# A decoder layer on one core: sixteen of the weight splits, and the gate factor of one branch, from VectorE to GpSimd

## The chip, the cores and the metric

The kernel runs on one core of a Trainium2 chip. The metric is the device time of one execution in microseconds (us). A core has TensorE (PE, matmuls, with its weight loads PEld), VectorE (DVE), ScalarE (ACT), GpSimd (POOL) and SyncE (SP, which here issues most DMA transfers). Each engine takes its instructions in the order in which they stand in its own queue and waits on semaphores for the others.

## The reference

One layer of a decoder trunk over 512 tokens of width 1024, all in float32:

```
h = rms_norm(x)
u = h @ w_in                     # 11512 columns: DSA, NSA, SSD inputs, three gates
y_a = dsa(u), y_b = nsa(u), y_c = ssd(u)     # three causal token mixers
mix = sig(g_a) * (y_a @ w_br_dsa) + sig(g_b) * (y_b @ w_br_nsa) + sig(g_c) * (y_c @ w_br_ssd)
x = x + mix @ w_out
x = x + square(relu(rms_norm(x) @ w_ff1)) @ w_ff2
```

DSA and NSA are attentions over selected keys (1024 wide each); SSD is a state-space mixer in four chunks of 128 tokens (2048 wide), and its output passes through an RMS norm with a gain of its own before the branch product.

## The kernel before

**Every product of matrices is three matmuls.** A float32 operand is split into a high half (rounded to the matmul's format, `F32R`) and a low half (the rest). `mm3` (L458 to L461) adds high x high, high x low and low x high in one PSUM bank. Activations are split once; weights are split as they stream in. The class `WS` holds the stream: a list of 190 and more weight pieces ("specs") in the order of use, each 128 x 1024 numbers at most. `load` fetches a piece into one of three raw buffers (`wraw`, issued on SP at L154); `split` makes the high half with a copy on ACT (L173) and the low half with a subtraction (L175), on DVE, except for the specs named in the set `LOWP`, whose low half POOL makes. The tiles `whi` and `wlo` have six buffers each, and splits run three specs ahead of use.

**The order of use.** Numbers of the specs: 0 to 67 are the projections of the mixers' inputs, 68 to 91 the 24 gate columns ("mg"), 92 to 99 the first branch (DSA output, a0), 100 to 107 and 108 to 115 the two halves of the third branch (SSD output, c0 and c1), then the second branch (NSA output, b0 and b1), `w_out` and the feed-forward weights.

**Two streams of work** are woven together: the mixers (DSA attention, then SSD, then NSA), whose matmuls are small and wait for softmaxes and exponentials, and the filler (projections, gates, branches), whose matmuls are 24 of 128x512 per output tile. The emission order is by a running balance of their costs; after that a scheduler with a model of each engine's times sets the order of instructions on every engine. So a change of engine for some instructions moves others too.

**SSD (about 400 to 570 us)** handles 16 units (group, chunk). For a unit POOL masks the decay exponents in a tile E (affine select, L1342), makes scaled inputs (xt L1347, xw L1350), adds (eab L1364), scales the state (hst L1373) and sums squares (yv, sq, L1390 and L1391). ACT takes exponentials of E (L1345), DVE multiplies E by a product that TensorE left in the single PSUM bank pv (L1352), and TensorE multiplies E with xt (L1312). After the NSA queries' norms POOL takes four powers (rs8, L1791). At the end four small matmuls (L1420) sum the squares, and the norm factors, one for each token, go through DRAM into the tile R (`rtok`), 128 x 512.

**The branches** (`branches`). For each of 8 output tiles m of a branch a gate tile (`gld`, 128 x 512, two buffers) is loaded by SP. It holds the hyperbolic tangent t; the sigmoid is (1 + t)/2, and the half is taken later. For the third branch the gate is first multiplied by the norm factor: `th = (th + 1) * R`, one instruction on DVE (L1564). TensorE makes the branch product p in a PSUM bank pj (two buffers), DVE takes `th * p` (L1589), and POOL adds this to the sum `mixf` (L1590), which frees the gate buffer. POOL also issues the loads of the queries for NSA (`qu <- q_d`, L1043, four buffers), each of which waits until TensorE has used the buffer's old contents.

Of the kernel before, what the change touches and what calls it, by code (L numbers as in the profile page):

```python
# [10 lines left out]
ALU = mybir.AluOpType  # L11
# [12 lines left out]
NS = 6  # L24
RAWB = 3
LEAD = 3
LOWP = {0} | set(range(8, 14)) | set(range(17, 24))
WE = 2
NH = 4
BH = 2  # L30
# [11 lines left out]
def build_kernel(ctx, tc, A, out):  # L42
    nc = tc.nc
    pe, act, dve, pool = nc.tensor, nc.scalar, nc.vector, nc.gpsimd
# [8 lines left out]
    def f(ap):  # L53
        return ap.bitcast(F32)
# [37 lines left out]
    def ps(tag, shape, dt=F32, bufs=2):  # L92
        if tag == XT[0]:
            XT[1] += 1
            if XT[1] % 3 == 0:
                tag = "pF"
        return psp.tile(shape, dt, tag=tag, name=tag, bufs=PSB[tag])
# [36 lines left out]
    class WS:  # L134
# [24 lines left out]
        def split(s):  # L159
# [14 lines left out]
            with tc.issue_after(H0[0][1]) if i == 1 else nullcontext():  # L174
                (pool if i in LOWP else dve).tensor_tensor(lo[:, :m], r[:, :m], f(hi[:, :m]), op=ALU.subtract)  # L175
            s.hl[i] = (hi[:, :m].rearrange("p (a b) -> p a b", b=w), lo[:, :m].rearrange("p (a b) -> p a b", b=w))
# [281 lines left out]
    def mm3(o, lh, ll, rh, rl, first, last):  # L458
        pe.matmul(o, lh, rh, start=first, stop=False)  # L459
        pe.matmul(o, lh, rl, start=False, stop=False)  # L460
        pe.matmul(o, ll, rh, start=False, stop=last)  # L461
# [39 lines left out]
    def proj_ch(i, rh, rl, p, first=True, last=True):  # L501
        wh, wl = ws.get(i)
        nk = ws.specs[i][1]
        for k in range(nk):
            mm3(p, wh[:, k, :], wl[:, k, :], rh(k), rl(k), first and k == 0, last and k == nk - 1)
            if k % 2 == 1:
                if k == nk - 1:
                    ws.free(i)
                yield 6 * 216
# [189 lines left out]
    def filler():  # L699
# [114 lines left out]
        while ya is None:  # L814
            yield None
            if "att2" in done:
                ya = first_ya()
        pclose("hT")
        yield from branches(ya)

    def load_y(yp, br, kk):
# [615 lines left out]
    def branches(ya):  # L1437
        bp = popen("br")
        mix = bp.tile([128, KT, S], F32, name="mixf")
        R = bp.tile([128, S], F32, name="rtok")  # L1440
# [9 lines left out]
        def load_g(n):  # L1450
            if n < len(seq) and n not in th_:
                br, m = seq[n]
                bi = "abc".index(br[0])
                c0, c1 = COLS.get(br, (0, S))
                if br[0] == "b":
                    gcnt[0] += 1
                g_ = R if br[0] == "b" and gcnt[0] % 3 == 0 else bp.tile([128, S], F32, name="gld", bufs=2)
                r0 = (bi * 8 + m) * 128
                if br in COLS:
                    g_ = g_.rearrange("p (a q) -> p a q", a=2)  # L1460
                    nc.sync.dma_start(g_, g_d[r0:r0 + 256, c0:c1].rearrange("(a p) q -> p a q", p=128))
                    th_[n], th_[n + 1] = g_[:, 0], g_[:, 1]
                else:
                    nc.sync.dma_start(g_, g_d[r0:r0 + 128])
                    th_[n] = g_

        def load(br, ks, pl):
            return [load_y(ypools[pl], br, kk) for kk in ks]
# [11 lines left out]
        for bi, br in enumerate(BR):  # L1480
# [54 lines left out]
            for m in range(8):  # L1535
                load_g(8 * bi + m)
                load_g(8 * bi + m + 1)
                if br in COLS and m % 2 == 0:
                    load_g(8 * bi + m + 2)
                    load_g(8 * bi + m + 4)  # L1540
                elif br == "b0":
                    load_g(8 * bi + m + 2)
                th = th_.pop(8 * bi + m)
                if br in ("a0", "c0", "c1") and m in (0, 6):
                    for m_ in (m, m + 1):
                        pp[m_] = ps("pj", [128, 512])
                    for half in range(2):
                        for m_ in (m, m + 1):
                            wi = P["br_" + br][m_]
                            wh, wl = ws.get(wi)  # L1550
                            for k in range(4 * half, 4 * half + 4):
                                mm3(pp[m_], wh[:, k, :], wl[:, k, :], yh[k], yl[k], k == 0, k == 7)
                            if half:
                                ws.free(wi)
                            yield 12 * 216
                        if m and not half:
                            nb_ = BR[bi + 1]
                            if nb_ == "c0":
                                while "yc" not in done:
                                    yield None  # L1560
                            if nb_ != "b0" or "nsa0" in done:
                                nxt = load(nb_, range(KS[nb_][0], KS[nb_][0] + 4), "A")
                if br[0] == "c":
                    dve.scalar_tensor_tensor(th, th, 1.0, R, op0=ALU.add, op1=ALU.mult)  # L1564
                if m in pp:
                    p = pp.pop(m)
                else:
                    p = ps("pj", [128, 512])
                    if br[0] == "b":
                        wi = P["br_b1" if br == "b2" else "br_" + br][m // 2]  # L1570
                        wh, wl = ws.get(wi)
                        ms = slice(128 * (m % 2), 128 * (m % 2) + 128)
                        for k in range(4):
                            mm3(p[:, :c1 - c0], wh[:, k, ms], wl[:, k, ms], yh[k][:, c0:c1], yl[k][:, c0:c1], k == 0, k == 3)
                            if k % 2:
                                if k == 3 and m % 2 and br != "b1":
                                    ws.free(wi)
                                yield 6 * (c1 - c0) / 2.37
                    else:
                        yield from proj_ch(P["br_" + br][m], lambda i: yh[i], lambda i: yl[i], p)  # L1580
                p = p[:, :c1 - c0]
                mx = mix[:, m, c0:c1]
                if br == "a0":
                    dve.scalar_tensor_tensor(mx, th, 1.0, p, op0=ALU.add, op1=ALU.mult)
                    continue
                if br[0] == "b":
                    dve.scalar_tensor_tensor(th, th, 1.0, p, op0=ALU.add, op1=ALU.mult)
                else:
                    dve.tensor_tensor(th, th, p, op=ALU.mult)  # L1589
                (dve if br in ("b1", "b2") else pool).tensor_tensor(mx, mx, th, op=ALU.add)  # L1590
                if br == "b2":
                    act.activation(mixh[:, m], mix[:, m], AF.Copy, scale=0.5)
                    dve.scalar_tensor_tensor(mixl[:, m], mix[:, m], 0.5, f(mixh[:, m]), op0=ALU.mult, op1=ALU.subtract)
# [264 lines left out]
```

## Time and profile before

| what | value |
|---|---|
| median of 3 runs | 1357.51 us (1356.02 to 1357.94) |
| the profiled execution | 1353.4 us |
| its span, first to last instruction | 1351.7 us |
| TensorE clock granted, mean | 0.995 |
| low halves on DVE, 128x1024 (raw piece from `wraw`) | 176, 223.6 us |
| low halves on POOL, 128x1024 | 9, 21.8 us |
| gate factors on DVE (L1564) | 16 |

The profile is of one execution. A row of an engine counts instructions that work on data; issuing a DMA, waiting and branching do not count as busy. A row names the line, the engine, the operation and `out<-in`. In a list of waits a row reads: the engine and tile that waited, the line, who released it, us in total, how many times, and the longest. A busy TensorE is not a TensorE at its peak, since the ends of matmuls are modelled. In a timeline, what stands in brackets is the engine's idle time ahead of the row and what ended it.

### The profile page before, as it was taken

To read this page: it belongs to the slowest core of one execution; us is meant where nothing else is said; L and a number is where in the kernel's file an instruction comes from. 1 tells how busy PE (TensorE), PEld (TensorE's weight loads), DVE (VectorE), ACT (ScalarE), POOL (GpSimd) and SP (SyncE) were. 2 spreads that over 40 slices of the span, in tenths; PEclk is the share of its full clock that TensorE was granted. 3 is DMA by queue.
4 is the path that set the end of the run, shared out by engine and by line. 5 is a ranking of instruction groups with operands and counts; after the bars stand their busy time and mean duration, and the time that the engine had idled before them with its cause. 6 is when DMAs were issued, how large, how long until landed. Compare 5 with 4: busy or idle time off the path is not lost.

```text
span 1351.7 us, 19620 instructions
## 1 busy us (share of the span) xinstructions
PE 1329.2 (98%) x6827; PEld 1111.0 (82%) x6827; DVE 994.2 (74%) x1971; ACT 728.3 (54%) x1395; POOL 272.0 (20%) x242
## 2 busy tenths in 40 slices
PE   9999999999999999999999999998999999999998
PEld 7788888888887777788888888887789888888887
DVE  6499986989977665467778889898655666767741
ACT  5455334677767775446665656556433443444420
POOL 2415111111006769500000112130000201102000
PEclk9999999999999999999999999999899999999999
DMA  6436665455559998663454545352427656746531
GB/s 199 120 88 170 189 179 137 123 159 144 146 149 347 304 295 289 193 187 102 118 164 119 167 136 145 117 168 94 156 66 188 132 160 132 179 114 127 150 125 47
DMA packets 251778, 213.74 MB, mean 158 GB/s; under 512 B 15882, under 2 KB 203166, under 8 KB 251679
## 3 DMA queue, kind: packets, MB, share of 16 engines
q1 hardware_dynamic: 235708, 188.88, 46.5%
q0 software_dynamic: 15232, 20.98, 8.2%
q10 hardware_dynamic: 738, 2.63, 0.5%
q8 instruction: 54, 0.88, 0.3%
q14 instruction: 46, 0.37, 0.1%
HBM read 171.75 MB, written 40.70 MB: 157 GB/s over the span
## 4 chain that ended last, share of the span: by engine, by line
PE 86%; DVE 4%; POOL 3%; ACT 2%; DMA 2%; issue 2%; SPq 0%; DVEq 0%; ACTq 0%; POOLq 0%
PE pj L459 20%; PE pj L460 20%; PE pj L461 20%; PE sc L461 3%; PE sc L459 3%; PE sc L460 3%; PE pT L984 3%; PE pv L997 2%; PE pv L996 2%; PE sc L925 2%; PE sc L924 2%; PE sc L1312 1%; POOL rs L1791 1%; DVE wlo L175 1%; PE pF L984 1%
## 5 line engine op out<-in xcount | busy, mean ns | idle before, releaser
L173 ACT ACTIVATE whi<-wraw 128x1024 fp32r<-128x1024 f32 (+2 forms) x190 | 198.3, 1046 | 238.0 <-PE pj L460 121.4
L175 DVE TENSOR_TENSOR wlo<-wraw,whi 128x1024 fp32r<-128x1024 f32 (+1 forms) x176 | 223.6, 1272 | 104.2 <-ACT whi L173 101.2
L459 PE MATMUL pj<-hTh,whi 128*128 128x512 f32 x512 | 203.5, 397 | 2.0 <-DVE cacc L853 2.0
L460 PE MATMUL pj<-hTl,whi 128*128 128x512 f32 x512 | 202.4, 395 | 0.0
L461 PE MATMUL pj<-hTh,wlo 128*128 128x512 f32 x512 | 202.2, 395 | 0.0
L933 ACT ACTIVATE p<-p,nb,rs 128x256 f32<-128x256 f32 (+3 forms) x160 | 107.8, 677 | 45.9 <-DVE nb L931 45.7
L459 PEld LDWEIGHTS pj<-hTh,whi 128*128 128x128 f32 x512 | 96.3, 188 | 20.9 <-ACT eab L1341 2.2
L460 PEld LDWEIGHTS pj<-hTl,whi 128*128 128x128 f32 x512 | 96.4, 188 | 19.2 <-issue 1.0
L461 PEld LDWEIGHTS pj<-hTh,wlo 128*128 128x128 f32 x512 | 96.3, 188 | 19.0 <-issue 0.2
L460 PE MATMUL pj<-yl,whi 128*128 128x512 f32 (+1 forms) x288 | 107.9, 375 | 0.0
L459 PE MATMUL pj<-yh,whi 128*128 128x512 f32 (+1 forms) x288 | 107.1, 376 | 0.8 <-ACT yh L1477 0.4
L461 PE MATMUL pj<-yh,wlo 128*128 128x512 f32 (+1 forms) x288 | 106.8, 372 | 0.0
L460 PE MATMUL pj<-h2l,whi 128*128 128x512 f32 (+1 forms) x256 | 96.4, 377 | 0.0
L461 PE MATMUL pj<-h2h,wlo 128*128 128x512 f32 (+1 forms) x256 | 96.3, 376 | 0.0
L459 PE MATMUL pj<-h2h,whi 128*128 128x512 f32 (+1 forms) x256 | 96.2, 377 | 0.0
L459 PE MATMUL pj<-whi,hTh 128*128 128x512 f32 (+2 forms) x208 | 80.0, 385 | 3.2 <-DVE v_s L561 2.2
L460 PE MATMUL pj<-wlo,hTh 128*128 128x512 f32 (+2 forms) x208 | 80.4, 387 | 0.0
L461 PE MATMUL pj<-whi,hTl 128*128 128x512 f32 (+2 forms) x208 | 79.8, 384 | 0.0
L988 ACT ACTIVATE pth<-pT 128x512 fp32r<-128x512 f32 x95 | 54.7, 592 | 43.5 <-PE pT L984 42.7
L1043 POOL DMA_DIRECT2D qu<-q_d x32 | 23.5, 736 | 264.4 <-PE sc L925 186.5
L989 DVE TENSOR_TENSOR ptl<-pT,pth 128x512 fp32r<-128x512 f32 x95 | 63.7, 679 | 4.4 <-ACT pth L988 4.3
L459 PE MATMUL sc<-whi,fh 128*128 128x512 f32 x168 | 65.4, 389 | 0.0
(410 smaller groups left out, 3155.7 us busy)
## 6 DMA issues: line engine op xcount, KB each, us to landing
wraw<-in_w_in_dram SPq DMA_DIRECT2D x84, 512.0 KB, 4.2
wraw<-in_w_ff_dram SPq DMA_DIRECT2D x58, 512.0 KB, 4.1
qd<-in_w_ff_dram POOLq DMA_DIRECT2D x18, 512.0 KB, 5.9
gld<-g_d SPq DMA_DIRECT2D x35, 256.0 KB, 2.7
q_d<-qev SPq DMA_DIRECT2D x64, 128.0 KB, 3.6
qu<-q_d POOLq DMA_DIRECT2D x32, 256.0 KB, 4.8
E<-ac_d SPq DMA_DIRECT2D x16, 512.0 KB, 6.1
xz<-xzt_d SPq DMA_DIRECT2D x16, 512.0 KB, 4.4
```

The lines of the kernel that those rows point to most:

```text
L173: act.activation(hi[:, :m], r[:, :m], AF.Copy)
L175: (pool if i in LOWP else dve).tensor_tensor(lo[:, :m], r[:, :m], f(hi[:, :m]), op=ALU.subtract)
L459: pe.matmul(o, lh, rh, start=first, stop=False)
L460: pe.matmul(o, lh, rl, start=False, stop=False)
L461: pe.matmul(o, ll, rh, start=False, stop=last)
L924: pe.matmul(s_[:, h % w, :n], u.q[h], kh[:, :n], start=True, stop=False)
L925: pe.matmul(s_[:, h % w, :n], u.q[h], kl[:, :n], start=False, stop=True)
L933: act.activation(u.p[h][:, :n], u.p[h][:, :n], AF.Exp, bias=u.nb[:, h:h + 1], scale=rs8[:, u.b, u.h0 + h:u.h0 + h + 1], accum_out=u.sm[:, ...
L984: pe.transpose(pt[:, h], u.p[h][:, kb * 128:kb * 128 + 128], ident)
L988: act.activation(ph, ptf, AF.Copy)
L989: dve.tensor_tensor(pl, ptf, f(ph), op=ALU.subtract)
L996: pe.matmul(o, vk, ph0, start=st, stop=False)
```

## The change

```diff
-LOWP = {0} | set(range(8, 14)) | set(range(17, 24))
+LOWP = {0} | set(range(8, 14)) | set(range(17, 24)) | set(range(70, 116, 3))
...
                 if br[0] == "c":
-                    dve.scalar_tensor_tensor(th, th, 1.0, R, op0=ALU.add, op1=ALU.mult)
+                    pool.tensor_tensor(th, th, R, op=ALU.mult)
+                    pool.tensor_tensor(th, th, R, op=ALU.add)
```

First, the low half of specs 70, 73, ... 115, sixteen in all, is made by POOL and not by DVE: 8 of the gate columns, 2 of the first branch and 6 of the third. Second, the third branch's gate times norm factor is made on POOL, by two instructions, `th * R` and then `+ R`, for each of its 16 tiles. Lines behind L1564 have numbers one higher in the new file. The instructions before and after each are the same, but the scheduler gives all engines another order from about 500 us on.

POOL in the second half of SSD, before; E_5160 is the decay tile of one unit, xt_5256 belongs to the unit before, rs8 are the four powers:

```order
L1390 TENSOR_TENSOR yv_5151<-yv_5151 128x256
L1364 TENSOR_TENSOR eab_5113<-eab_5113,xz_5051 128x512
L1391 TENSOR_TENSOR sq0_4087<-sq0_4087,yv_5151 128x256
L1347 TENSOR_TENSOR xt_5256<-xs_5162,sv_dth_1818 128x512
L1373 TENSOR_TENSOR hst_5135<-hst_5135,sv_dec_1821 128x512
L1350 TENSOR_TENSOR xw_5320<-xs_5236,sv_dw_1820 128x512
L1364 TENSOR_TENSOR eab_5168<-eab_5168,xz_5109 128x512
L1342 AFFINE_SELECT E_5160<-E_5160 128x1024
L1791 TENSOR_TENSOR rs8_316<-ssn_317,mhalf_164 128x16 x4
```

The same place after the change, from the add eab_5113 on:

```order
L1364 TENSOR_TENSOR eab_5113<-eab_5113,xz_5051 128x512
L175 TENSOR_TENSOR wlo_6038<-wraw_5816,whi_6037 128x1024
L1347 TENSOR_TENSOR xt_5256<-xs_5162,sv_dth_1818 128x512
L1792 TENSOR_TENSOR rs8_316<-ssn_317,mhalf_164 128x16 x4
L1390 TENSOR_TENSOR yv_5151<-yv_5151 128x256
L1373 TENSOR_TENSOR hst_5135<-hst_5135,sv_dec_1821 128x512
L1364 TENSOR_TENSOR eab_5168<-eab_5168,xz_5109 128x512
L1350 TENSOR_TENSOR xw_5320<-xs_5236,sv_dw_1820 128x512
L1347 TENSOR_TENSOR xt_5318<-xs_5236,sv_dth_1818 128x512
L1391 TENSOR_TENSOR sq0_4087<-sq0_4087,yv_5151 128x256
L175 TENSOR_TENSOR wlo_6244<-wraw_6041,whi_6243 128x1024
L1342 AFFINE_SELECT E_5160<-E_5160 128x1024
```

The powers moved from behind the select of E_5160 to ahead of it, xt_5318 too, and two splits came in ahead of it (a third, wlo_5813, stands five rows above those shown).

POOL in the third branch, before; the numbers of `gld` tell the gate tiles apart, `qu` are query loads:

```order
L1043 DMA qu_8127<-q_d3_2_71 128x2x256
L1043 DMA qu_8129<-q_d3_2_71 128x2x256
L1590 TENSOR_TENSOR mixf_7585<-mixf_7585,gld_8224 128x512
L1590 TENSOR_TENSOR mixf_7585<-mixf_7585,gld_8248 128x512
L1590 TENSOR_TENSOR mixf_7585<-mixf_7585,gld_8393 128x512
L1590 TENSOR_TENSOR mixf_7585<-mixf_7585,gld_8398 128x512
L1590 TENSOR_TENSOR mixf_7585<-mixf_7585,gld_8465 128x512
L1043 DMA qu_8933<-q_d3_1_70 128x2x256
```

And after, from the second add of a gate's norm factor on:

```order
L1565 TENSOR_TENSOR gld_8248<-gld_8248,rtok_7586 128x512
L175 TENSOR_TENSOR wlo_8548<-wraw_8296,whi_8547 128x1024
L1591 TENSOR_TENSOR mixf_7585<-mixf_7585,gld_8224 128x512
L1591 TENSOR_TENSOR mixf_7585<-mixf_7585,gld_8248 128x512
L1564 TENSOR_TENSOR gld_8394<-gld_8394,rtok_7586 128x512
L1564 TENSOR_TENSOR gld_8400<-gld_8400,rtok_7586 128x512
L1043 DMA qu_8129<-q_d3_2_71 128x2x256
L1565 TENSOR_TENSOR gld_8394<-gld_8394,rtok_7586 128x512
L1565 TENSOR_TENSOR gld_8400<-gld_8400,rtok_7586 128x512
L1591 TENSOR_TENSOR mixf_7585<-mixf_7585,gld_8394 128x512
```

A query load that stood ahead of all adds of the branch now stands between the multiplies and the adds of two gate tiles, and splits stand among them.

## The prediction

> **What bounds the kernel now.** I read the page first, then the busy time by stage, then what TensorE waits for in each stage, then the chain of waits around the places that the change touches. The page:
>
> ```profile
> span 1351.7 us, 19620 instructions
> PE 1329.2 (98%) x6827; PEld 1111.0 (82%) x6827; DVE 994.2 (74%) x1971; ACT 728.3 (54%) x1395; POOL 272.0 (20%) x242
> ```
>
> TensorE is busy for all but 22.5 us, so the whole kernel is a queue of matmuls, and a gain can come only from those gaps. I cut the span where the work changes: 490 to 570 us is the end of the SSD mixer, 570 to 690 gate projections beside NSA attention, 690 to 850 the first and third branch beside NSA, 850 to 970 the second branch and the end of NSA. Columns: us, PE, PEld, DVE, ACT and POOL busy with counts, clock, DMA.
>
> ```profile
> 490.00:570.00 80.00, 78.05 (x435) 62.21 (x436) 47.81 (x57) 47.68 (x99) 62.34 (x48) 1.00 0.80 257
> 570.00:690.00 120.00, 120.00 (x609) 100.55 (x609) 84.29 (x235) 70.97 (x152) 5.79 (x8) 1.00 0.48 140
> 690.00:850.00 160.00, 159.94 (x823) 135.24 (x821) 138.01 (x324) 98.17 (x196) 20.82 (x17) 1.00 0.50 143
> 850.00:970.00 120.00, 111.64 (x638) 96.76 (x637) 103.87 (x278) 71.42 (x165) 19.61 (x15) 0.96 0.40 122
> ```
>
> From 570 to 850 us, where 12 of the 16 moved splits and nearly all the moved gate factors lie, TensorE idles for 0.06 us, although VectorE is 86% busy (138.01 of 160) in the second half. Freeing VectorE there cannot shorten anything directly. The gaps lie before and after, and the waits of TensorE name them, first 490 to 570 us, then 850 to 970 us (us in total, times, longest).
>
> ```profile
> PE pv L1312 <- DVE E L1352: 0.7, 1, 0.7
> PE pF L619 <- DVE qev L623: 0.6, 1, 0.6
> PE sc L1312 <- DVE eab L1363: 0.4, 1, 0.4
> ```
>
> ```profile
> PE pv L996 <- ACT pth L988: 2.1, 1, 2.1
> PE pv L1152 <- DVE yr L1007: 2.0, 1, 2.0
> ...
> PE pv L1152 <- DVE yt L1014: 0.7, 1, 0.7
> ...
> ```
>
> So 1.7 us are open in the SSD stage and 4.8 us in these three rows of the tail. One sign that VectorE is near to mattering in between: the chain of waits passes through its queue from about 797 us and gives TensorE a start at 820.77 with nothing to spare.
>
> ```profile
> 818.32 0.84 DVE wlo L175
> 819.44 0.67 DVE gld L1564
> 820.11 0.61 DVE gld L1589
> 820.77 0.50 PE pj L459
> ```
>
> **The change part by part.** What one of each costs, first the low halves (ns least/median/largest on DVE; on POOL busy us and mean ns), then the gate factor on DVE, and the nearest POOL row to its replacement, an add of two 128x512 fp32 tiles in SBUF.
>
> ```profile
> L175 DVE TENSOR_TENSOR wlo<-wraw,whi x176: 1097/1220/3486, 11.0 to 1324.7; 128x1024 fp32r<-128x1024 f32 x173, 128x912 fp32r<-128x912 f32 x3
> L175 POOL TENSOR_TENSOR wlo<-wraw,whi 128x1024 fp32r<-128x1024 f32 x9 | 21.8, 2437 | 37.2 <-ACT whi L173 36.7 <-POOL wlo L175 0.6
> L1564 DVE SCALAR_TENSOR_TENSOR gld<-gld,rtok x16: 670/678/694, 755.7 to 872.6; 128x512 f32<-128x512 f32 x16
> L1590 POOL TENSOR_TENSOR mixf<-mixf,gld x22: 1281/1295/2276, 765.6 to 920.0; 128x512 f32<-128x512 f32 x22
> ```
>
> Sixteen splits leave DVE: 16 x 1.22 = 19.5 us; on POOL they are 16 x 2.44 = 39.0 us. Sixteen factors leave DVE: 16 x 0.68 = 10.8 us; on POOL each is a multiply and an add, 16 x 2 x 1.295 = 41.4 us. DVE loses 30.3 us, POOL gains 80.4 us. None of it is on TensorE's path as long as TensorE's waits stay as they are, so the sum is made of what happens to those waits, stage by stage.
>
> SSD stage (490 to 570 us). Five splits (specs 70, 73, 76, 79, 82) come onto POOL here, 5 x 2.44 = 12.2 us into 17.7 us of idle time (80 less 62.34). The order puts three of them, the four powers and one more multiply (xt) ahead of the select that makes E_5160. The rows that time this today, POOL, DVE and PE:
>
> ```profile
> 512.87 1.54 POOL L1342 TENSOR_SCALAR_AFFINE_SELECT E<-E 128x1024 f32<-128x1024 f32 x1
> 514.39 12.51 POOL L1791 TENSOR_TENSOR rs<-ssn,mhalf 128x16 f32<-128x16 f32 x4
> 528.24 1.04 POOL L1347 TENSOR_TENSOR xt<-xs,sv_dth 128x512 f32<-128x512 f32 x1
> ```
>
> ```profile
> 517.79 1.21 DVE L1352 TENSOR_TENSOR E<-E,pv 128x1024 f32<-128x1024 f32 x1
> ```
>
> ```profile
> 519.81 0.38 PE L1312 MATMUL pv<-bcx 128*128 128x128 f32 x2
> 526.70 1.09 PE L1312 MATMUL sc<-E,xt 128*64 128x128 f32 x16 [0.41 <-DVE eab L1363]
> ```
>
> ```profile
> 1150.00:1200.00 50.00, 50.00 (x222) 41.45 (x221) 36.01 (x40) 22.23 (x25) 4.91 (x4) 1.00 0.61 148
> ```
>
> Today the select starts at 512.87, its product with the decay (read from the one pv bank) ends at 519.0, and TensorE's next matmul into that bank stands at 519.81: 0.8 us to spare. After the change the select is behind 12.5 (powers) + 1.0 (xt) + 3 x 2.44 (splits) = 20.8 us more: near 533.7, and its product ends 6.1 us on, at 539.8. TensorE gets there later too: counted from the last row that both orders share, 130 projection matmuls stand ahead of that pv matmul where 50 stood, 80 x 0.225 us (50 us over 222) = 18.0 us, so at 537.8. That is a wait of 2.0 us in place of 0.8 us to spare, less what POOL's gaps take in (17.7 us are idle in the stage). Bounds: -1.7 us if all three waits of the stage go, +7.6 us if the three splits are also stretched as the worst add was (2276 over 1295 ns in the row above, 3 x 2.44 x 0.76 = 5.6 us). I take +1.0 us, between the 2.0 and the 0.7 of today's wait of the same kind (pv behind the product), to which it is nearest.
>
> Middle (570 to 850 us). The weights: a POOL split ends about 1.2 us later than a DVE split, and so frees its raw buffer later; three splits of lead, each 24 matmuls of 0.225 us (5.4 us), cover that, and on SP the load of the next raw tile and what is queued behind it (gate loads, stores of attention output) move by the same 1.2 us under the same cover. The gates: one gate buffer's round is load, factor, product, add, and the load is the page's row:
>
> ```profile
> gld<-g_d SPq DMA_DIRECT2D x35, 256.0 KB, 2.7
> ```
>
> Before 2.7 + 0.68 + 0.68 + 1.3 = 5.4 us, now 2.7 + 2.6 + 0.68 + 1.3 = 7.3 us, for two buffers 3.6 us per output tile against 5.4 us of matmuls per tile: hidden. What can bring it out is POOL's order. POOL also issues the query loads, and one of those (qu_8129) now stands between the multiplies and the adds of two gates. It waits for TensorE to free a query buffer, and such waits are long (570 to 850 us):
>
> ```profile
> POOL qu L1043 <- PE sc L925: 128.8, 6, 28.6
> ```
>
> Today nothing urgent is queued behind them. Now a late query load holds the add, the add holds the product on DVE (L1590 of the new file waits for POOL), and behind that product stand NSA's maxima and exponent biases. Against that, DVE gets slack. How much of it stays is told by how the two engines run side by side, DVE then POOL:
>
> ```profile
> 765.71 4.62 DVE L175 TENSOR_TENSOR wlo<-wraw,whi 128x1024 fp32r<-128x1024 f32 x2
> ```
>
> ```profile
> 765.57 2.53 POOL L1590 TENSOR_TENSOR mixf<-mixf,gld 128x512 f32<-128x512 f32 x2
> ```
>
> Two splits that cost 2.44 us alone took 4.62 us beside two POOL adds of 2.53 us: DVE lost 2.2 us, nearly all of POOL's time. DVE's instructions of this kind, two inputs in SBUF, from 570 to 850 us:
>
> ```profile
> L175 DVE TENSOR_TENSOR wlo<-wraw,whi 128x1024 fp32r<-128x1024 f32 x35 | 44.8, 1283 | 11.3 <-ACT whi L173 10.9 <-DMA g_d<-gth 0.3
> L829 DVE SCALAR_TENSOR_TENSOR yl<-yl,gcol,yh 128x512 fp32r<-128x512 f32 x16 | 12.3, 783 | 1.6 <-ACT yh L828 1.6
> ```
>
> With 11 splits left on POOL here (11 x 1.28 = 14.1 us off the first row) these two rows are 43.0 us of 280, 15%. POOL's new 41.4 + 11 x 2.44 = 68 us then block DVE for about 0.15 x 68 = 10 us, out of 14.1 + 10.8 = 24.9 us won: some 40% is handed back. [...] The page "Perfetto Trace Analysis" of the Trainium skill, section "Optimizing Scalar/DVE Operations", warns that for this reason moving work between the two might not help; by that rule the sum of this stage would be nil or a loss. By the rows it is nil too, since nobody waits for DVE here: bounds 0 and the loss under the rivals; I take +0.
>
> Tail (850 to 970 us). No split or factor of this stage moves, but the order on TensorE does. Now 29 branch matmuls of 128x256 stand in TensorE's order between the last score matmuls (L946) and the pv matmuls that wait (L1152); after the change 48, the same matmuls otherwise. Their pace (24 rows, first and last), the last scores and the waits:
>
> ```profile
> 929.38 0.28 PE L459 MATMUL pj<-yh,whi 128*128 128x256 f32 x1
> 932.12 0.28 PE L461 MATMUL pj<-yh,wlo 128*128 128x256 f32 x1
> 935.99 0.28 PE L946 MATMUL sc<-kl_j,qu 128*128 128x256 f32 x1
> 942.89 0.72 PE L984 MATMUL pF<-ident,p 128*128 128x128 f32 x3 [1.37 <-DVE p L970]
> 944.33 0.50 PE L1152 MATMUL pv<-cph,vz 128*128 128x256 f32 x2 [0.72 <-DVE yt L1014]
> 948.45 0.48 PE L1152 MATMUL pv<-cph,vz 128*128 128x256 f32 x2 [1.99 <-DVE yr L1007]
> ```
>
> 19 x 2.74/23 = 2.3 us more cover for waits of 1.37 + 0.72 + 1.99 = 4.1 us that follow from those scores through softmax, transposes and yr. Bounds 0 (what limits them is queued elsewhere) and -2.3 us; I take half, -1.1 us.
>
> Sum: +1.0 + 0 - 1.1 = -0.1. The profiled execution took 1353.4 us, 1.7 us beyond its span; by the sum it would take 1353.3. The runs shown have a median of 1357.51, 4.1 us above it, and I set the change against that: 1357.4 us.
>
> **The rivals.** (1) Faster: the 1.7 us of SSD waits go, because two of the three are waits for DVE's queue, which loses splits there, and the tail gets its full 2.3 us: -4.0 us, 1353.5. For it speaks that each wait named is on DVE; against it, the powers and splits now ahead of the select.
> (2) Slower, in the middle: POOL becomes late. The place is the product L1590 of the new file, 16 times, with NSA's chain behind it and TensorE without slack as at 820.77. If each costs TensorE 0.5 us, +8 us, 1365.5. It decides from the point where DVE's loss eats its gain: blocking above 24.9/68 = 37% of POOL's new time (15% by the rows above), or query loads that hold an add longer than the 5.4 us of one tile. For it: 138.01 of 160 us busy on DVE, and the queue order. Against it: POOL would still be only near 80 of 160 us busy.
> (3) Slower, in the SSD stage: the splits on POOL are stretched by DVE beside them, and TensorE waits 2.0 us and half of the 5.6 us for the pv bank, nothing coming back before the next stage: with the tail at -1.1, +3.7 us, 1361.2. For it: POOL is 78% busy there (62.34 of 80) before 12.2 us are added. Against it: the order has already moved 80 matmuls in front.
>
> **How the numbers follow.** A change of under 0.2% (2.7 us) is about what a measurement of this kernel can tell from none. My forecast, within that, 0.40; rival 1 0.30; rival 2 0.15; rival 3 0.15. So faster 0.30, same 0.40, slower 0.30. The forecast's own range is 1354.8 to 1360. The range for 8 in 10 reaches to both near rivals, 2 us past rival 1 for a tail whose first wait (2.1 us) goes too, and into the lower half of rival 2: 1351.5 to 1363.5.
>
> **What would show it right or wrong.** Right: TensorE idle again near 22 us, nil between 570 and 850; POOL busy near 350 us; DVE busy down by 15 to 25 us and not by 30, with L175 on DVE beside POOL stretched; a wait of pv or sc L1312 near 535 us of at most 2 us; the waits before L1152 shorter. Wrong: TensorE waits with a DVE product or POOL gld as releaser between 690 and 850 us (rival 2), one wait of 4 us or more near 535 us (rival 3), or a tail without its two or three waits (rival 1).

## The result, and the profile after

| | median, us | runs |
|---|---|---|
| before | 1356.76 (1353.84 to 1357.94) | 4 |
| after | 1371.70 (1368.88 to 1377.24) | 4 |
| ratio | 1.0118, 95% interval 1.0079 to 1.0158 | |

The change makes the kernel slower by 1.2%, some 15 us, where the forecast was no change and the range ended at 1363.5 us. A second series of the same kernel gave 1.0123 (1.0107 to 1.0139). The profiled execution took 1373.88 us, so the two profiles lie somewhat farther apart (20.5 us) than the medians (14.9 us). Its page:

```profile
span 1372.2 us, 19644 instructions
PE 1336.8 (97%) x6827; PEld 1110.6 (81%) x6827; DVE 997.0 (73%) x1939; ACT 729.5 (53%) x1395; POOL 351.4 (26%) x290
```

POOL is where the prediction put it (351.4 us, forecast near 350). DVE is not: 30 us of work left it and its busy time rose from 994.2 to 997.0 us. TensorE idles 1372.2 - 1336.8 = 35.4 us where it idled 22.5, so 12.9 of the 20.5 us by which the span grew are open gaps. The other 7.6 us count as busy, for the same 6827 matmuls at a mean clock of 0.996 (0.995 before). Added up, the durations of these matmuls are 2469.0 us before and 2469.6 us after, so the matmuls are not longer: they overlap less. A matmul that is listed at 0.39 us follows the one before it after 0.225 us (50 us over 222 matmuls), so a wait of under some 0.17 us opens no gap. That the 7.6 us are such short waits is a guess that no run here tests.

The same stretches as before (us, then PE, PEld, DVE, ACT and POOL busy):

```profile
490.00:570.00 80.00, 75.80 (x436) 60.51 (x433) 43.93 (x48) 47.28 (x98) 63.97 (x49) 1.00 0.83 258
570.00:690.00 120.00, 119.25 (x603) 99.64 (x602) 81.32 (x213) 67.98 (x143) 23.24 (x18) 1.00 0.48 139
690.00:850.00 160.00, 150.26 (x749) 124.46 (x748) 129.43 (x294) 91.93 (x189) 59.23 (x41) 0.99 0.46 132
850.00:970.00 120.00, 111.69 (x612) 93.02 (x610) 107.78 (x276) 72.16 (x171) 41.42 (x30) 0.99 0.41 123
```

Idle time grew by 2.25 us in the SSD stage (from 1.95 to 4.20), by 0.75 from 570 to 690, by 9.7 in the middle (from 0.06 to 9.74), and not at all in the tail (8.31 against 8.36). The stage in which I had costed everything at nothing made most of the new idle time. Who ended TensorE's longest waits from 690 to 990 us (total, times, longest):

```profile
PE sc L924 <- DVE mx L926: 4.2, 5, 1.9
PE pj L459 <- DVE gld L1590: 3.0, 1, 3.0
PE pv L1152 <- DVE yr L1007: 2.8, 1, 2.8
PE pv L997 <- DVE ptl L989: 2.0, 4, 1.4
PE pj L460 <- DVE yl L829: 1.7, 2, 1.0
```

In these five rows every releaser is DVE; the next one is a wait of 1.5 us for ACT (pth, 2.1 us before). Three of the five are new, the tail's wait for yr was there with 2.0 us, and that for ptl with 0.6:

```profile
PE pv L997 <- DVE ptl L989: 0.6, 1, 0.6
```

DVE in turn waits for POOL's gate in only one place from 690 to 870 us:

```profile
DVE gld L1590 <- POOL gld L1565: 1.4, 1, 1.4
```

That wait ended at 784.40 us, and TensorE has no idle time between 771 and 804 us. So a late POOL queue is not what TensorE waits for. What slows DVE is seen in the durations of instructions that nobody moved. First before, then after, 690 to 990 us, by shape (busy us, mean ns):

```profile
L175 DVE TENSOR_TENSOR wlo<-wraw,whi 128x1024 fp32r<-128x1024 f32 x35 | 47.3, 1354 | 2.6 <-ACT whi L173 2.5
L829 DVE SCALAR_TENSOR_TENSOR yl<-yl,gcol,yh 128x512 fp32r<-128x512 f32 x16 | 12.3, 783 | 1.6 <-ACT yh L828 1.6
L931 DVE SCALAR_TENSOR_TENSOR nb<-mx,rs 128x4 f32<-128x4 f32 x19 | 3.4, 179 | 0.2
```

```profile
L175 DVE TENSOR_TENSOR wlo<-wraw,whi 128x1024 fp32r<-128x1024 f32 x26 | 42.1, 1617 | 0.0
L829 DVE SCALAR_TENSOR_TENSOR yl<-yl,gcol,yh 128x512 fp32r<-128x512 f32 x16 | 16.8, 1068 | 5.0 <-ACT yh L828 5.0
L931 DVE SCALAR_TENSOR_TENSOR nb<-mx,rs 128x4 f32<-128x4 f32 x19 | 9.2, 483 | 0.3
```

Nine splits left DVE here (35 to 26), and only 5.2 us went with them (47.3 to 42.1). The third row is the one to look at. `nb` is the exponent's bias of an NSA unit, 128x4 numbers, a link of the chain scores, maximum (L926), bias (L931), exponential on ACT (L933). It took 0.18 us on average and takes 0.48. One of them, DVE and then POOL:

```profile
791.08 2.14 DVE L931 SCALAR_TENSOR_TENSOR nb<-mx,rs 128x4 f32<-128x4 f32 x1
```

```profile
790.82 2.37 POOL L175 TENSOR_TENSOR wlo<-wraw,whi 128x1024 fp32r<-128x1024 f32 x1
```

POOL's split began 0.26 us earlier and ended at 793.19; the little instruction ended at 793.22. It did 0.15 us of work (its median before is 150 ns) and stood for the rest of POOL's instruction, and the exponentials stood behind it. Six of the 19 took over 0.25 us after the change (one before), and each of the six began while POOL was inside a split, a multiply of a gate or an add to `mixf`.

This one held up no matmul: TensorE isn't idle near 793 us. The longest wait of the middle, 3.0 us, has the same picture in front of it. TensorE, then DVE, then POOL:

```profile
770.86 0.50 PE L459 MATMUL pj<-yh,whi 128*128 128x512 f32 x1 [3.00 <-DVE gld L1590]
```

```profile
767.38 2.10 DVE L1127 TENSOR_SCALAR ib<-ib 128x8 f32<-128x8 f32 x1
769.52 0.69 DVE L1130 TENSOR_TENSOR smask<-ib,caus 128x512 f32<-128x512 f32 x1
770.12 0.68 DVE L1590 TENSOR_TENSOR gld<-gld,pj 128x512 f32<-128x512 f32 x1
```

```profile
767.10 2.35 POOL L175 TENSOR_TENSOR wlo<-wraw,whi 128x1024 fp32r<-128x1024 f32 x1 [1.65 <-ACT whi L173]
```

An instruction on 128x8 numbers, 0.17 us before the change, stood until POOL's split ended, and the product that TensorE's matmul waits for stood behind it. It has one tensor input, so not only instructions with two are held up. Of TensorE's seven waits of more than 0.1 us between 690 and 850 us (9.7 us together) five, with 6.9 us, have such a held-up DVE instruction at most two rows ahead of the releaser or as the releaser itself (L1127, L175 and three of yl L829). Ahead of the other two, 1.9 and 0.8 us, DVE had itself been idle for 1.6 and 2.4 us, waiting for ACT's yh.

### The profile page after: what moved, and what is told of

Read it like the earlier page. It is cut to its first block, busy times and chain, and to the rows that moved or that the text cites. A ratio compares the mean times of both kernels' runs of the same rounds, so it can differ in the third digit from the quotient of the medians.

```text
span 1372.2 us, 19644 instructions
## 1 busy us (share of the span) xinstructions
PE 1336.8 (97%) x6827; PEld 1110.6 (81%) x6827; DVE 997.0 (73%) x1939; ACT 729.5 (53%) x1395; POOL 351.4 (26%) x290
## 4 chain that ended last, share of the span: by engine, by line
PE 85%; DVE 7%; DMA 3%; ACT 2%; issue 2%; POOL 0%; SPq 0%; DVEq 0%; ACTq 0%; POOLq 0%
PE pj L459 20%; PE pj L460 20%; PE pj L461 20%; PE sc L459 3%; PE sc L461 3%; PE sc L460 3%; PE pT L984 2%; PE sc L924 2%; PE sc L925 2%; PE pv L996 2%; PE pv L997 2%; PE sc L1312 1%; DVE wlo L175 1%; ACT p L933 1%; DMA yl<-yc_d 1%
## 5 line engine op out<-in xcount | busy, mean ns | idle before, releaser
L175 DVE TENSOR_TENSOR wlo<-wraw,whi 128x1024 fp32r<-128x1024 f32 (+1 forms) x160 | 208.0, 1301 | 93.4 <-ACT whi L173 91.2
L933 ACT ACTIVATE p<-p,nb,rs 128x256 f32<-128x256 f32 (+3 forms) x160 | 108.3, 680 | 72.5 <-DVE nb L931 72.4
L175 POOL TENSOR_TENSOR wlo<-wraw,whi 128x1024 fp32r<-128x1024 f32 (+2 forms) x30 | 68.6, 2292 | 125.5 <-ACT whi L173 125.0
L459 PEld LDWEIGHTS pj<-yh,whi 128*128 128x128 f32 x288 | 55.1, 192 | 14.3 <-DVE gld L1590 3.1
```

The lines of the kernel that those rows point to most:

```text
L933: act.activation(u.p[h][:, :n], u.p[h][:, :n], AF.Exp, bias=u.nb[:, h:h + 1], scale=rs8[:, u.b, u.h0 + h:u.h0 + h + 1], accum_out=u.sm[:, ...
```

## The experiments

Three theories went in. **A, the port:** a POOL instruction that reads SBUF holds up DVE's instructions with two inputs there, and where such an instruction is a link of NSA's chain, TensorE waits. **B, the late start:** POOL's longer work in SSD starts NSA later, and its end stands alone. **C, the queue:** DVE waits for POOL's gate factor. Below are all 18 kernels at a glance, two of them timed twice; "idle" is TensorE's idle time from 690 to 990 us (the stretches 690 to 870 and 870 to 990 added), "NSA" the start of the first and the last score matmul of L1084. Ratios are of many executions, idle time is of one, which can lie some us from the median (e16 was profiled at 1357.98 us, its median is 1362.08).

| kernel | ratio to before (95%) | idle, us | NSA, us |
|---|---|---|---|
| before | | 8.4 | 585.4 to 890.8 |
| the change | 1.0118 (1.0079 to 1.0158) | 19.3 | 596.8 to 912.4 |
| a2_change_again | 1.0123 (1.0107 to 1.0139) | 18.6 | 596.3 to 911.4 |
| e1_splits | 1.0034 (1.0023 to 1.0044) | 11.2 | 596.9 to 899.9 |
| e2_gates | 1.0055 (1.0040 to 1.0070) | 11.6 | 586.9 to 905.8 |
| e3_ssd | 1.0063 (1.0048 to 1.0078) | 10.1 | 596.0 to 904.1 |
| e4_late | 0.9963 (0.9947 to 0.9979) | 4.7 | 590.6 to 884.0 |
| e4b_late_again | 0.9947 (0.9934 to 0.9959) | 4.5 | 586.8 to 880.0 |
| e5_extra_reads | 1.0038 (1.0020 to 1.0057) | 12.3 | 587.7 to 898.3 |
| e6_extra_fills | 0.9996 (0.9980 to 1.0012) | 8.1 | 587.9 to 893.7 |
| e7_mult_only | 1.0003 (0.9985 to 1.0020) | 7.4 | 586.4 to 896.8 |
| e8_powers_twice | 1.0103 (1.0073 to 1.0134) | 14.1 | 598.9 to 915.1 |
| e9_late_gates | 0.9995 (0.9978 to 1.0012) | 7.4 | 588.0 to 883.6 |
| e10_ssd_gates | 1.0122 (1.0108 to 1.0136) | 15.2 | 595.6 to 915.1 |
| e11_later | 0.9975 (0.9962 to 0.9988) | 6.1 | 588.4 to 882.0 |
| e12_sixteen_later | 1.0090 (1.0075 to 1.0104) | 15.6 | 587.4 to 892.2 |
| e14_after_mulpow | 1.0057 (1.0044 to 1.0070) | 9.3 | 586.0 to 884.5 |
| e15_before_mulpow | 1.0010 (1.0001 to 1.0019) | 7.5 | 575.3 to 884.4 |
| e16_late_add | 1.0050 (1.0038 to 1.0063) | 9.1 | 583.5 to 885.8 |
| e17_gate_fills | 1.0006 (0.9990 to 1.0022) | 5.9 | 594.3 to 891.3 |

With idle time at 14 us or more the time is 0.9% to 1.2% above before, at 8.4 us or less within 0.1% of it or below. Two of the six kernels in between, e14 and e16, have further gaps earlier.

**The two parts alone.** Splits only, and gates only:

```diff
 e1  LOWP = ... | set(range(70, 116, 3))
 e2  - dve.scalar_tensor_tensor(th, th, 1.0, R, op0=ALU.add, op1=ALU.mult)
     + pool.tensor_tensor(th, th, R, op=ALU.mult)
     + pool.tensor_tensor(th, th, R, op=ALU.add)
```

> Only the sixteen splits go to POOL, the gate factors stay on DVE. Theory A (the port: each added POOL instruction holds back DVE's instructions with two SBUF inputs, and late NSA steps then hold TensorE; the price goes with the POOL time added beside NSA): 27 of the 75 us of POOL time that lies behind 570 us are splits, so about a third of the loss of 15 us, +5 us; DVE's stretching in 690 to 870 us a third of what the full change shows. Theory B (late start: five splits in the SSD stage move the start of NSA by 11 us, and TensorE's order has no room for that): +12 to +15 us, as the full change. Theory C (the queue: DVE stands waiting for POOL's gate factors): 0.

> Only the gate factors go to POOL (32 instructions), all splits stay as before. Theory A: 48 of the 75 us of POOL time behind 570 us, about +10 us, with DVE busy nearly as before although 11 us of work left it. Theory B: 0, since SSD and the start of NSA are untouched (start of the first NSA score matmul as before within 1 us). Theory C: +15 us, the whole loss, with DVE waits on POOL's gate tiles of several us in the list.

Measured 1359.21 us beside 1354.12 (+0.34%) and 1361.45 beside 1354.12 (+0.55%). Both cost, and together 0.89%, less than the whole. The splits are at A's figure, the gates below it. In e2 DVE is busy for 997.7 us (994.2 before), although 10.8 us of work left it. C is weak already: the gates alone cost about 7 us and not 15, and from 690 to 870 us no wait of DVE for POOL's gate is listed in e2.

**The splits by place.** The five of the SSD stage, and the eleven later ones:

```diff
 e3  LOWP = ... | set(range(70, 83, 3))
 e4  LOWP = ... | set(range(85, 116, 3))
```

> Only the five splits that fall into the SSD stage (70 to 82) go to POOL. Theory A: about 0 to +2 us, since little of POOL's new time lies beside NSA. Theory B: NSA starts some 10 us later and the kernel loses +12 us or more. Theory C: 0.

> Only the eleven later splits (85 to 115) go to POOL, SSD is untouched. Theory A: 27 of the 75 us, about +4 us. Theory B: 0, and the start of NSA as before. Theory C: 0.

Measured 1362.47 us (+0.63%) and 1348.28 us (-0.37%), beside 1354.12. The five cost more than all sixteen and the eleven gain. For B speaks that e3 starts NSA 10.6 us later, though it lost some 8 us and not the 12 that B gave it; e4 is below what any theory gave it. None had counted what a shorter DVE queue may gain; that this is what e4 gains is not shown. A repeat of e4 beside later kernels:

> The eleven late splits alone once more, beside the three other kernels: -0.37% (-5 us) as the first time (0.9947 to 0.9979), if it is no accident of that chip; within 0.15% of no change otherwise.

1348.46 us beside 1355.65 (-0.53%): it holds, and it is the fastest kernel of the study.

**Reads or time on POOL.** The kernel before with extra POOL work, written behind each gate factor: four small products that read SBUF, or nine fills that read nothing. The scheduler moved all of it ahead of the first gate factor: the 64 products run from 697.5 to 758.0 us, the 144 fills from 687.1 to 745.8.

```diff
 e5  + for _ in range(4): pool.tensor_tensor(dum, R[:, 0:256], R[:, 256:512], op=ALU.mult)
 e6  + for _ in range(9): pool.memset(dum, 0.5)
```

> The kernel before, gate factors on DVE, with four POOL multiplies of 128x256 out of SBUF behind each gate factor, into a scratch tile that nobody reads: about 46 us of POOL time more, as the gate factors on POOL take (48 us), but nothing waits for them except POOL's own adds behind them. Theory A (a POOL instruction that reads SBUF holds back DVE's two-input instructions through the shared port): DVE is stretched by some 12 us more in 690 to 870 us and, with the gate factors still on DVE, the loss is at least that of the gates alone, +7 us or more. Theory C (waiting for POOL's results or the order of POOL's queue is the cost): the loss is under +3 us, DVE's durations as before.

> The same, but with nine POOL fills of 128x256 (no read of SBUF) in place of the four multiplies: about the same POOL time, and nearly the same order on all engines. Theory A with the narrow rule (only a POOL instruction that reads SBUF holds back DVE's two-input instructions): 0 to +2 us, DVE's durations as before. Theory A with the wide rule (any POOL instruction takes the port): as the run with the reads. Theory C: as the run with the reads, since POOL's queue is as full.

Measured 1360.18 us (+0.38%) and 1354.30 (-0.04%), beside 1355.36. The stretch 690 to 770 us in e5, with two groups of DVE in it, then the same of e6:

```profile
690.00:770.00 80.00, 77.24 (x396) 64.43 (x395) 72.86 (x160) 46.69 (x99) 57.57 (x67) 1.00 0.50 147
...
L970 DVE TENSOR_SCALAR p<-p,rc 128x384 f32<-128x384 f32 x9 | 6.3, 732 | 0.1
...
L931 DVE SCALAR_TENSOR_TENSOR nb<-mx,rs 128x4 f32<-128x4 f32 x6 | 1.7, 288 | 0.1
```

```profile
690.00:770.00 80.00, 80.00 (x421) 68.22 (x420) 66.00 (x169) 50.53 (x103) 48.84 (x143) 1.00 0.53 151
...
L970 DVE TENSOR_SCALAR p<-p,rc 128x384 f32<-128x384 f32 x9 | 4.1, 487 | 0.1
...
L931 DVE SCALAR_TENSOR_TENSOR nb<-mx,rs 128x4 f32<-128x4 f32 x6 | 0.9, 152 | 0.1
```

POOL is busy for 57.6 and 48.8 of the 80 us. Beside the reads nb takes 288 ns and TensorE idles for 2.8 us; beside the fills nb takes 152 ns (150 before) and TensorE doesn't idle. Over the whole kernel the reads add 55.8 us of POOL and the fills 47.4, and DVE is busy for 1005.9 us beside the reads, 993.4 beside the fills and 994.2 before. This is A, with a loss of some 5 us where A gave 7 or more, and it doesn't depend on POOL being late, because nothing waits for `dum`. The Trainium skill, page "SBUF — State Buffer", section "Who interferes with whom", says that a VectorE instruction with two SBUF inputs contends with a GpSimd instruction that reads SBUF and not with one that only writes it. These two runs agree for nb, an instruction with two inputs, and the wide rule of the expectation (any POOL instruction takes the port) does not stand for it.

**Half the gate's work on POOL** (the multiplication alone; the addition of R is left out, so the gate is another number):

```diff
 e7  + pool.tensor_tensor(th, th, R, op=ALU.mult)
```

> The gate factor on POOL as one multiply; the add of R is left out, so the gate of the third branch is t * R in place of (1 + t) * R. POOL has 16 instructions and some 24 us less than with the whole factor. Theory A: about half of the loss of the gates alone, +3 to +4 us, and DVE stretched half as much more. Theory C (latency of the gate tile's round): nearly nil, since the round is then 6.0 us for two tiles.

1356.50 us (+0.03%), below what A gave it; C had given it nil. nb is stretched here too (330 ns from 690 to 990 us). So the cost is not proportional to POOL's reading time, and a stretched nb is a sign of the blocking and not a measure of the loss.

**POOL's time in SSD without any split.** The four powers taken twice:

```diff
 e8  + for _ in range(2):
           pool.tensor_tensor(rs8[:, b, 16:32], ssn[:, b], mhalf[:, :16], op=ALU.pow)
```

> The kernel before with POOL's four powers of the NSA norms taken twice: 12 us more of POOL time in the SSD stage, about what the five splits there add, and no split moved. Theory B (what the splits 70 to 82 cost is that POOL's chain in SSD is longer, NSA starts late and ends late): NSA's first score matmul some 10 us later and +6 to +9 us in all, as with those splits. Rival (the splits themselves, by what TensorE or DVE wait for them): under +3 us.

1369.20 us beside 1355.36 (+1.03%), above the figure of B. NSA starts 13.5 us later, and idle time from 870 to 990 us is 13.0 us (8.4 before). Twelve us more of POOL's time in SSD are dear with no split moved.

**Parts in pairs, and four more late splits.**

```diff
 e9   gates on POOL, LOWP = ... | set(range(85, 116, 3))
 e10  gates on POOL, LOWP = ... | set(range(70, 83, 3))
 e11  LOWP = ... | set(range(85, 128, 3))
```

> The gates and the eleven late splits (specs 85 to 115) on GpSimd, the five SSD splits on VectorE. If the parts simply add (gates +0.55%, late splits -0.37%): +0.18%, about +2.4 us. If the parts come in each other's way where they meet, between 740 and 890 us, with the 0.37% by which the whole change (+1.18%) is above the sum of its parts (+0.81%): +0.55%, about +7.5 us, with small VectorE instructions (nb, L931) stretched at least as much as in the whole change. If the late start is what makes the rest dear, this kernel, which starts NSA early, is at +0.2% or below.

> The gates and the five SSD splits on GpSimd, the eleven late splits on VectorE. If the parts add (gates +0.55%, SSD splits +0.63%): +1.18%, about +16 us, which is as much as the whole change. If the gates and the late splits are what comes in each other's way: also +1.18%, while the kernel with late splits and gates is dear. If a late start makes the gates dearer: above +1.18%, near +1.5%.

> Fifteen late splits (specs 85, 88, ... 127) on GpSimd, nothing else: four more than in the late kernel, from the first half of the second branch. If what the late splits win is VectorE's time in the last stretch of NSA (850 to 990 us), four more win more there: -0.45% to -0.6%. If they win by another order alone, or the shared port costs VectorE as much as it wins there: -0.1% to -0.37%.

Measured beside 1355.65 us: 1354.91 (-0.05%), 1371.97 (+1.22%), 1352.18 (-0.25%). Gates and SSD splits add (0.55 + 0.63 = 1.18) and make the whole loss. The eleven late splits gain 0.4% to 0.5% alone, take away the cost of the gates in e9, and are worth nothing in the whole change. Four more lose half of their gain. The loss doesn't always stand in the middle: in e10 TensorE idles for 3.7 us from 690 to 870 us and for 11.5 us from 870 to 990 (8.4 before). In e9 POOL is busy for 77.5 us between 690 and 870 us, more than in the change (70.6 us), and TensorE idles there for 1.1 us against 11.3: POOL's busy time doesn't tell what it costs.

**Place or number.**

```diff
 e12  gates on POOL, LOWP = ... | set(range(85, 116, 2))
```

> Gates and sixteen splits on GpSimd as in the change, but the sixteen are specs 85, 87, ... 115: none in SSD. If the place in SSD costs: within 0.3% of before (the late splits with the gates are at 0.9995), NSA's last score (L1084) before 893 us. If it is the number of instructions that GpSimd takes: +0.9% or more, since GpSimd has as much more work as in the change, all of it in a shorter stretch.

1366.05 us beside 1354.50 (+0.90%), with NSA starting at 587.4 us. My reading that only the place in SSD costs falls. Here TensorE idles for 11.4 us between 690 and 870, and its waits from 690 to 990 us name another DVE instruction, the scaling of p (L970):

```profile
PE pF L984 <- DVE p L970: 7.3, 5, 4.2
PE pT L984 <- DVE p L970: 2.6, 2, 1.7
```

**POOL's time in SSD taken away again.** The four powers become additions of the same tiles, in the changed kernel (e14) and in the one before (e15); the norm factors of the NSA queries, and what follows, are other numbers.

```diff
 e14, e15  - pool.tensor_tensor(rs8[:, b, 16:32], ssn[:, b], mhalf[:, :16], op=ALU.pow)
           + pool.tensor_tensor(rs8[:, b, 16:32], ssn[:, b], mhalf[:, :16], op=ALU.add)
```

> The changed kernel, but the four powers of the NSA queries' norms (L1792, 12.5 us of GpSimd) are replaced by additions of the same tiles, so the norm factors and what follows from them are other numbers. If GpSimd's time in SSD decides, the 12.2 us of the five splits are made up for, NSA starts near 585 us and the time falls back to that of gates and late splits, -0.3% to +0.3% of before. If the splits cost by their place in another way (VectorE held up, TensorE's waits for the select), it stays at +0.8% or above.

> The kernel before with the same replacement of the four powers. If GpSimd's time in SSD decides at every amount: NSA starts about 8 us earlier and the time falls by 0.4% to 0.8%. If the filler's work is the bound once NSA starts at 585 us: -0.2% to 0.

1362.78 us (+0.57%) and 1355.33 (+0.10%), beside 1354.50. With the 12 us back the change loses half as much, not nothing: between the two expectations. And an NSA that starts 10 us early (575.3 us) gains nothing: e15 lies just above both of its expectations.

**Relief of POOL in SSD on top of the late splits:** the add L1364 on DVE.

```diff
 e16  e4 and  - pool.tensor_tensor(t1, t1, u.xd, op=ALU.add)
              + dve.tensor_tensor(t1, t1, u.xd, op=ALU.add)
```

> The eleven late splits on GpSimd, and SSD's add eab <- eab, xz (L1364, 12 times 1.48 us of GpSimd) on VectorE (12 times about 0.68 us). If relief of GpSimd in SSD still pays: -0.6% or better against before. If VectorE's longer queue there costs as much, or nothing is to be had by an earlier NSA: -0.45% to -0.2%, as the late splits alone.

1362.08 us beside 1354.50 (+0.50%): the gain of e4 is gone, a miss for both. From 490 to 690 us TensorE idles for 5.7 us here (1.95 before), and I did not follow it further.

**The change without the gates' reads.** Two fills of the gate tile in place of multiply and add, with all its waits and hand-overs; the norm factor and the gate's numbers are left out. The change itself stands beside it.

```diff
 e17  - pool.tensor_tensor(th, th, R, op=ALU.mult)
      - pool.tensor_tensor(th, th, R, op=ALU.add)
      + pool.memset(th, 0.5)
      + pool.memset(th, 0.5)
```

> The changed kernel once more. If its order decides which VectorE instructions meet which GpSimd ones, the idle time of TensorE between 690 and 870 us (11.3 us the first time) and the stretch of nb (L931, mean 483 ns from 690 to 990 us) come again within a third, and the time is at +1.0% to +1.3%.

> The changed kernel with the two gate instructions (th times R, plus R) replaced by two fills of the same gate tile, which read nothing from SBUF: the norm factor and the gate's numbers are left out. About 0.6 us each in place of 1.3 to 1.5; every wait and hand-over of the gate tile stays. If the port is what costs: nb (L931) falls back below 300 ns, TensorE's idle time from 690 to 870 us below 5 us, and the time to that of the splits alone (+0.34%, up to +0.7%). If the order of the work, and not the reads, is what costs: still +0.9% or more, idle above 8 us.

1372.34 us (+1.23%) and 1354.76 (+0.06%), beside 1355.43. From 690 to 870 us, the change again and then the fills:

```profile
690.00:870.00 180.00, 168.43 (x843) 138.49 (x841) 149.02 (x320) 100.91 (x205) 70.14 (x47) 0.99 0.43 126
```

```profile
690.00:870.00 180.00, 180.00 (x929) 152.66 (x928) 145.99 (x360) 111.58 (x228) 58.88 (x57) 1.00 0.47 137
```

The idle time is 11.6 us in this second profile of the change (11.3 in the first), so it belongs to the order and is no accident. Without the reads it is zero, and the whole loss is gone, though the sixteen splits are still on POOL. nb did not fall under 300 ns as expected (337 on average from 690 to 990 us), because two of them still meet a split and one an add to `mixf`; L1127 is back at 0.17 us. Three things changed at once here: the reads went, each gate takes about 1.1 us of POOL (546 and 538 ns) in place of 3.0, and a few instructions stand in another order. Since e7, with one reading instruction for each gate, lost nothing either, e17 alone can't tell the reads from the time; only e5 and e6 do. And NSA starts at 594.3 us, nearly as late as in the change, and ends where it ended before:

```profile
L1084 PE MATMUL sc<-kc,qu x64: 191/277/278, 594.3 to 891.3; 128*128 128x64 f32 x64
```

A late start is therefore not a price by itself. In the change the same row runs from 596.8 to 912.4.

**What follows.** A holds for the middle: adding reads makes a loss and fills make none (e5, e6), with the gates' reads gone the loss is gone (e17), and DVE instructions held up by POOL stand ahead of five of the seven waits there. It is not the whole of it: with the five SSD splits gone and the gates' reads left (e9) the loss is gone as well, so the change needs both for its loss. C is contradicted, since DVE's wait for POOL's gate is 1.4 us in all, at a place where TensorE doesn't idle. B is half true: POOL's time in SSD costs (e3, e8), but only where NSA doesn't catch up later. What I read into that, that a DVE held up by POOL can't catch up while one with fewer splits can, fits e17, e9 and the change. It is argued and not shown; e8 with late splits was not tried. Nor does idle time account for all that the late start costs: in e3, e8 and e10 the span grew by 8.7, 14.8 and 19.7 us and TensorE's busy time by 6.3, 7.7 and 11.9 of them, which no run follows. Why sixteen later splits meet NSA's chain and eleven do not is open too.

## Why the prediction was wrong, point by point

- **What bounds the kernel:** TensorE is the busiest engine, and that was the trap. "TensorE idles for 0.06 us" in the middle was read as "nobody waits for DVE". It says only that DVE was in time, and not by how much. The row I quoted myself (a chain through DVE that gives TensorE a start at 820.77 with nothing to spare) was the better witness. And the premise that time lies only in the gaps was too narrow: 7.6 us of the growth count as busy.
- **Durations on POOL:** right for a split (2.43 us, forecast 2.44), somewhat low for the gates (1.45 + 1.53 = 2.98 us per tile, forecast 2.59). In the page's groups after:

```profile
L1565 POOL TENSOR_TENSOR gld<-gld,rtok 128x512 f32<-128x512 f32 x16 | 24.4, 1528 | 0.8
L1564 POOL TENSOR_TENSOR gld<-gld,rtok 128x512 f32<-128x512 f32 x16 | 23.2, 1453 | 42.1 <-DMA gld<-g_d 38.9 <-DMA yb_d<-yt 3.2
```

- **The blocking (the step that failed, first half):** I took DVE's share of time in two groups (15%) times POOL's new time, 10 us from 570 to 850 us. In those two groups it is 26 x 0.263 + 16 x 0.285 = 11.4 us from 690 to 990 us, and 21 x 0.092 + 16 x 0.285 = 6.5 us from 570 to 850, so for them the size was not too small. What I left out was everything small: nb alone grew by 19 x 0.304 = 5.8 us. By share of busy time nb was nothing (3.4 us of 300). A blocked instruction doesn't pay by its own length, it pays by the rest of the other engine's (0.15 us became 2.14, 0.17 became 2.10). Over the whole kernel DVE's busy time should have fallen by 30.3 us and rose by 2.8; these 33.1 us are 42% of the 79.4 us that POOL gained, where I had taken 15%.
- **Middle, "I take +0" (the step that failed, second half):** the blocking was set against the 24.9 us won, as if DVE's time were one purse. The wins fall on splits, which run three specs ahead of use, and for which no wait of TensorE is listed after the change. The losses fall on whatever meets POOL, and behind that stand products and maxima that TensorE does wait for. Measured: 9.7 us idle from 690 to 850 us, in place of 0.06.
- **Gate ring and order on POOL:** the ring was hidden as worked out. The query load that was to hold an add waited for nothing and took 0.76 us (from 782.27 us); DVE's one wait of 1.4 us came from two gate multiplies ahead of it that started late, after 3.6 us of waiting for a gate load. TensorE lost nothing by it.
- **SSD, "+1.0", bounds -1.7 to +7.6:** the stage lost 2.25 us, within the bounds by luck. The select that was to start near 533.7 started at 532.43, but TensorE waits for other tiles there, and not for the pv bank:

```profile
PE pF L619 <- DVE qev L623: 1.5, 1, 1.5
PE pj L459 <- ACT gth L795: 1.4, 1, 1.4
PE sc L1312 <- DVE yv L1381: 1.3, 1, 1.3
```

  The larger effect, the start of NSA 11.4 us later, was in no term. I had taken filler matmuls moved forward as harmless because TensorE stays busy.
- **Tail, "-1.1":** the three waits of 4.1 us did shrink to 3.0, as forecast, but not evenly: the first fell from 1.37 to 0.19 us, that for yt is gone, and that for yr is 2.8 us where it was 2.0, in spite of 19 more matmuls of cover. New waits in the same stretch (three for DVE's maxima, 1.27, 0.92 and 0.41 us) took the gain back: idle time is 8.31 us against 8.36.
- **DVE busy, "down by 15 to 25 us":** up by 2.8.
- **The rivals:** the second had the side, the place and one of its two mechanisms, and its price was too small: it gave 8 us and a chance of 0.15. Its turning point, blocking above 37% of POOL's new time, was passed (42% over the whole kernel). Its other mechanism, POOL late, was wrong, and so was what I held against it ("only near 80 of 160 us busy"): POOL at 59 of 160 us was enough. The first had the wrong sign; the third's wait for the pv bank didn't come. The rule on the page "Perfetto Trace Analysis" of the Trainium skill, section "Optimizing Scalar/DVE Operations", that moving work between the two engines might not help was dismissed because the rows of this stage gave nil "too". Those rows priced work and not waiting.

## What to carry to other kernels

Before moving work from DVE to POOL, list the small DVE instructions in front of what the busiest engine waits for, and price each meeting at the remainder of one POOL instruction (here up to 2 us for one of 0.15 us), not at a share of busy time. That gives what DVE loses; how much of it the busiest engine loses depends on what stands behind (e7 and e17 stretched nb to nearly twice its time and lost nothing). A stage in which the bound engine never idles may still have no room, when its releasers are just in time: look there for what is late next. Where parts of a change are separable, time them apart: here eleven of the splits alone are 0.4% to 0.5% faster than before, and the rest of the change turns that into 1.2% slower.

## What the runs showed of the hardware that was not expected

- A scaling with one tensor input (L970, `p * rc`, 128x384) is stretched beside POOL's reads as well: 732 ns in e5 against 487 in e6. The Trainium skill, page "SBUF — State Buffer", section "Who interferes with whom", names tensor_scalar among the operations that can enter a mode with both ports and then contend, if their operands meet its conditions; the trace agrees that it is held up.
- Fills on POOL cost next to nothing: 144 of them, 0.31 us each, left nb at 152 ns and the time at 0.9996 (0.9980 to 1.0012). But the scaling L970 (128x384) took a little longer beside them, 487 ns where it took 415 before in the same stretch (690 to 770 us):

```profile
L970 DVE TENSOR_SCALAR p<-p,rc 128x384 f32<-128x384 f32 x9 | 3.4, 415 | 0.1
```

- POOL is stretched too: the adds of the third branch (L1565) take 1.53 us on average where the shortest takes 1.29. The other way round, in e1, where the gates stay on DVE and the splits run on POOL, the factors on DVE take 0.80 us in place of 0.68.
